# Low parts of the streamed weights: a VectorE subtraction replaced by a negated copy on ScalarE and an accumulating DMA

## The chip, the cores and the metric

One Trainium2 chip; the kernel uses one core. The metric is the device time of one execution in microseconds (us), taken as the median of several executions. Lower is better. Beside the times there is one profiled execution, and all durations below come from its trace. The compute engines are TensorE (PE in the profile, with its weight loads as a row of their own, PEld), VectorE (DVE), ScalarE (ACT) and GpSimd (POOL); SyncE (SP) issues most of the DMAs, and 16 DMA engines carry them out. Each engine has its own list of instructions, whose order is fixed when the program is built.

## The reference

Two layers of a diffusion trunk in float32, on 1024 latent tokens and 256 context tokens of width 1024. Layer 0 is multi-head latent attention with 8 heads, layer 1 a Hyena long convolution. Cut to what matters:

```python
for i in range(2):
    shift, scale, gate = split(silu(c) @ ada_w[i] + ada_b[i], 3)
    a = rmsnorm(x, norm_g[i]) * (1 + scale) + shift        # and the same for the context in layer 0
    if i == 0:   # latent attention
        cq, ckv, k_rope, g = split(a @ mla_w_in)
        q, kv = rmsnorm(cq) @ w_uq, rmsnorm(ckv) @ w_ukv
        y = (softmax(q k^T * s) v * silu(g)) @ mla_w_out
    else:        # Hyena
        u, g = split(a @ hy_w_in)
        v, g0, g1 = split(depthwise_conv3(u))
        z = g0 * longconv(v);  z = g1 * longconv(z)        # filters from a small MLP
        y = (z * silu(g)) @ hy_w_out
    x = x + gate * y
return rmsnorm(x, final_g)
```

The large products with weights are `a @ mla_w_in`, `@ mla_w_out`, `a @ hy_w_in` and `@ hy_w_out`. All weights arrive in float32.

## The kernel before

Everything is kept transposed: features on the 128 partitions, tokens along the row. A product that needs more precision than one pass of TensorE gives is made of three: every operand x is split into a high part hi (x rounded to the type fp32r) and a low part lo = x - hi (again fp32r), and the method `mm3` (lines 117 to 121) adds hi*hi, hi*lo and lo*hi in PSUM. So line 119 uses the weight's high part with the activation's high part, line 120 the weight's high part with the activation's low part, and line 121 the weight's low part. `split` (lines 95 to 97) makes the two parts of any operand: ScalarE copies (line 96), VectorE subtracts (line 97).

The weights of the four large products are not kept in SBUF; they are streamed in **pieces** of 128 x 512 float32, 256 KB (some 128 x 256). `feed` (lines 99 to 103) opens a pool and lists the pieces in the order in which they will be used; `weights` (lines 105 to 115) is called by whoever needs the next piece, and makes pieces ahead of it. For each piece it asks for three tiles: `raw`, called wr in the profile, and the two parts, called w. A tile name with n buffers takes them in turn; whoever writes a buffer waits until the last reader of its earlier content is done. Before the change wr has 2 buffers, and each of the parts has 3, or 2 in the pool that `out_first` opens. The load of `raw` goes on SyncE's queue (line 112). `weights` keeps at most two pieces listed as loaded, one of which it hands out.

The framework orders the instructions of each engine when the program is built, by priority (the order of the program text) and a model of when each is ready; an instruction whose buffer is not free yet can be placed behind later ones. So the place of a piece's instructions among others is not only that of the call.

There are three feeds:

- **Layer 0's input** (`layer0_in`, lines 440 to 623): 34 pieces of `mla_w_in` (wr<-in_w). Each tile of 128 output features takes two pieces; each piece of the latent tokens serves two halves of 512 tokens, 24 matmuls. `project` (lines 410 to 425) is a generator, and the work on it is interleaved with the making of the Hyena filters (`filters`, lines 284 to 358) and with the adaLN products (`ada`, whose loads of ada_w are called aw and pg). GpSimd loads the matrices of the filters' transforms here (line 295), and later ckv and krh for the attention (lines 641 to 647).
- **The output projection, first half of the tokens** (`out_first`, lines 886 to 905): 16 pieces of `mla_w_out` (wr<-in_wo). It begins inside the last unit of the attention, and each piece serves one half of the tokens, 12 matmuls. The pool has two buffers for each part. Its matmuls write tiles called po. The attention output is loaded and split by `out_heads` (lines 865 to 876, og<-ograw).
- **The rest** (`layer0_out` and `hyena`, lines 908 to 1272): the same 16 pieces of `mla_w_out` for the second half of the tokens (12 matmuls each), 64 pieces of `hy_w_in` (wr<-in_hw, 24 matmuls each, interleaved with the long convolutions of the chunk before), 16 pieces of the first six eighths of `hy_w_out` (wr<-in_hoa, 24 and 12 matmuls in turn) and 8 of the last two eighths (wr<-in_hob, 12 matmuls each, the first four for one half of the tokens, the last four for the other, with the final norm's first sums between). While the second half of the output projection runs, GpSimd loads the transform matrices dm in four steps (lines 966 to 970); each step first copies one element of x of the tile before last (line 969).

The attention between the first two feeds takes no streamed pieces; its weights (wa, wb, wc) go through `split`, which the change leaves as it is.

Of the kernel before, what the change touches and what calls it, by code (L numbers as in the profile page):

```python
# [11 lines left out]
F32 = mybir.dt.float32  # L12
F32R = mybir.dt.float32r
AF = mybir.ActivationFunctionType
ALU = mybir.AluOpType
# [4 lines left out]
P = 128  # L20
# [35 lines left out]
class Net:  # L56
# [47 lines left out]

    def weights(self):

        while self.coming and len(self.loaded) < 2:
            ap = self.coming.popleft()
            n = ap.shape[-1]
            raw = self.wp.tile([P, 512], F32, tag="wr", name="wr", bufs=2)[:, :n]  # L110
            hi, lo = [self.wp.tile([P, 512], F32R, tag=f"w{r}", name="w")[:, :n] for r in range(2)]
            self.nc.sync.dma_start(out=raw, in_=ap)
            self.split(raw, hi, lo)
            self.loaded.append((hi, lo))
        return self.loaded.popleft()

# [1299 lines left out]
```

## Time and profile before

| | |
|---|---|
| median of 3 executions | 1739.24 us (1736.87 to 1746.16) |
| the profiled execution | 1735.72 us |
| its span, first to last instruction | 1733.9 us |
| granted TensorE clock, mean | 0.976 of full speed |
| lines 96 and 97 on streamed pieces | 154 each, 93.7 and 102.4 us busy |

In the profile a group of instructions is given as line, engine, operation, output<-input by the program's names, the shapes and a count; then its busy time, the mean duration in ns, and how long its engine sat idle just before these instructions, with what ended most of that. A wait is given as "who, tile, line <- whom: us in total, times, longest". L96, L97 and L119 to L121 are helper lines that serve many tiles, so they are read together with the tile's name. The chain is the sequence of work that ended last, followed back from the last instruction. A line of the stage table gives start:end, length, busy us and count of PE, PEld, DVE, ACT and POOL, the granted clock, the busy share of the DMA engines and their GB/s.

The stages in the trace: layer 0's input from 0 to about 430 us, attention to about 931, the output projection to about 1037, the norm and the Hyena layer from there, of which the last output projection and the final norm take the part from about 1650.

### The profile page before, as it was taken

The page shows a single profiled execution, that of the slowest core. Times are in us where ns is not written, and L with a number is a line of the kernel's source. Part 1 is how long each engine was busy: PE and PEld are TensorE (multiplying, and loading weights), DVE is VectorE, ACT ScalarE, POOL GpSimd, SP SyncE. Part 2 cuts the span into 40 slices and gives each one's busy share as a digit, 9 for nine tenths or more (in the row PEclk, how much of TensorE's full clock was granted, in tenths as well). Part 3 has the DMA queues.
Part 4 walks back from the last instruction along what each step waited for, and adds up shares of the span by engine and source line. Part 5 has one row for each costly group of instructions (what it writes and reads, how often), then busy time and mean ns, then how long its engine had stood idle before and what let it go on. Part 6 is the DMA issues. An engine that isn't in the chain of part 4 may idle for free.

```text
span 1733.9 us, 22766 instructions
## 1 busy us (share of the span) xinstructions
PE 1635.3 (94%) x8096; PEld 1300.2 (75%) x8096; DVE 1442.4 (83%) x2539; ACT 766.1 (44%) x1331; POOL 15.4 (1%) x43
## 2 busy tenths in 40 slices
PE   6799897898999999999999999999999999999995
PEld 2467676686788788788787777888888888887873
DVE  4885978895598899899889466999999999999856
ACT  4533444435455555455556345433433433433313
POOL 1000000000000000000000010000000000000000
PEclk8899998999999999999999999999999999999998
DMA  9777563436101001010013781332332332334555
GB/s 341 255 231 222 182 191 118 147 95 196 37 22 42 25 26 37 25 33 25 19 56 121 233 268 64 101 97 84 100 117 83 104 111 85 102 113 138 175 158 204
DMA packets 139030, 207.19 MB, mean 119 GB/s; under 512 B 13386, under 2 KB 67361, under 8 KB 138788
## 3 DMA queue, kind: packets, MB, share of 16 engines
q1 hardware_dynamic: 135780, 195.05, 35.7%
q0 software_dynamic: 3136, 10.69, 1.9%
q8 instruction: 64, 1.05, 0.2%
q14 instruction: 50, 0.41, 0.1%
HBM read 149.97 MB, written 53.61 MB: 117 GB/s over the span
## 4 chain that ended last, share of the span: by engine, by line
PE 79%; DMA 8%; DVE 8%; ACT 3%; issue 1%; SPq 1%; DVEq 0%; ACTq 0%
PE pj L121 13%; PE pj L119 13%; PE pj L120 12%; PE O L120 2%; PE S L119 2%; PE O L119 2%; PE S L811 2%; DMA kd<-ko 2%; PE O L121 2%; PE apx L747 2%; PE S L810 2%; PE S L121 2%; PE S L120 2%; PE apx L748 2%; DMA aw<-in_adaw 2%; PE fu L119 2%
## 5 line engine op out<-in xcount | busy, mean ns | idle before, releaser
L96 ACT CAST w<-wr 128x512 fp32r<-128x512 f32 (+1 forms) x154 | 93.7, 609 | 259.2 <-PE pj L120 134.3
L119 PE MATMUL pj<-a,w 128*128 128x512 f32 x512 | 203.3, 398 | 1.7 <-ACT a L407 1.6
L121 PE MATMUL pj<-a,w 128*128 128x512 f32 x512 | 203.3, 398 | 0.0
L120 PE MATMUL pj<-a,w 128*128 128x512 f32 x512 | 203.2, 397 | 0.0
L813 ACT ACTIVATE p<-S 128x512 f32<-128x512 f32 x160 | 95.5, 597 | 148.2 <-DVE acc L820 69.5
L97 DVE TENSOR_TENSOR w<-wr,w 128x512 fp32r<-128x512 f32 (+1 forms) x154 | 102.4, 673 | 56.5 <-ACT w L96 56.3
L96 ACT CAST bh<-raw 128x512 fp32r<-128x512 f32 x128 | 77.0, 620 | 88.8 <-DVE raw L1056 71.1
L119 PEld LDWEIGHTS pj<-a,w 128*128 128x128 f32 x512 | 96.5, 189 | 22.0 <-ACT a L407 2.4
L120 PEld LDWEIGHTS pj<-a,w 128*128 128x128 f32 x512 | 96.6, 189 | 19.8 <-DVE a L408 0.2
L121 PEld LDWEIGHTS pj<-a,w 128*128 128x128 f32 x512 | 96.7, 189 | 19.4 <-issue 0.8
L97 DVE TENSOR_TENSOR p<-p 128x512 fp32r<-128x512 f32 x160 | 109.5, 685 | 1.5 <-ACT p L96 1.2
L749 DVE TENSOR_REDUCE cm<-apx 128x1 f32<-128x512 f32 (+1 forms) x192 | 107.3, 592 | 3.8 <-PE apx L748 3.0
L121 PE MATMUL pj<-pg,w 128*128 128x512 f32 (+1 forms) x248 | 98.0, 395 | 9.5 <-DVE w L97 9.5
L820 DVE TENSOR_TENSOR acc<-acc,p 128x512 f32<-128x512 f32 x144 | 98.9, 687 | 7.6 <-ACT p L813 6.7
L96 ACT CAST p<-p 128x512 fp32r<-128x512 f32 x160 | 99.4, 622 | 4.8
L119 PE MATMUL pj<-pg,w 128*128 128x512 f32 (+1 forms) x248 | 96.7, 393 | 2.4 <-ACT pg L407 2.4
L120 PE MATMUL pj<-pg,w 128*128 128x512 f32 (+1 forms) x248 | 98.1, 396 | 0.6 <-DVE pg L408 0.6
L97 DVE TENSOR_TENSOR bl<-raw,bh 128x512 fp32r<-128x512 f32 x128 | 84.9, 688 | 9.1 <-ACT bh L96 8.9
L119 PE MATMUL u<-bh,fm 128*128 128x256 f32 (+1 forms) x200 | 67.8, 340 | 11.6 <-ACT bh L96 9.0
L321 DVE TENSOR_TENSOR kk<-ph,dec 128x512 f32<-128x512 f32 x64 | 42.9, 685 | 35.4 <-DMA dec<-in_dec 28.2
L747 PE MATMUL apx<-kn,qn 128*128 128x512 f32 (+1 forms) x192 | 69.1, 364 | 2.3 <-DVE cm L749 1.9
L748 PE MATMUL apx<-krh,r 128*128 128x512 f32 (+1 forms) x192 | 67.2, 358 | 0.0
(304 smaller groups left out, 4392.4 us busy)
## 6 DMA issues: line engine op xcount, KB each, us to landing
aw<-in_adaw SPq DMA_DIRECT2D x32, 512.0 KB
kd<-ko SPq DMA_DIRECT2D x128, 128.0 KB
wr<-in_hw SPq DMA_DIRECT2D x64, 256.0 KB
kt<-kd SPq DMA_DIRECT2D x56, 256.0 KB
wr<-in_w SPq DMA_DIRECT2D x34, 256.0 KB
dec<-in_dec SPq DMA_DIRECT2D x64, 128.0 KB
pg<-in_adaw SPq DMA_DIRECT2D x32, 256.0 KB
wr<-in_wo SPq DMA_DIRECT2D x32, 256.0 KB
```

The source lines that it names most:

```text
L96: self.nc.scalar.copy(out=hi, in_=raw)
L97: self.nc.vector.tensor_tensor(out=lo, in0=raw, in1=hi, op=ALU.subtract)
L119: mm(out, lhsT=w[0], rhs=x[0], start=start, stop=False)
L120: mm(out, lhsT=w[0], rhs=x[1], start=False, stop=False)
L121: mm(out, lhsT=w[1], rhs=x[0], start=False, stop=stop)
L321: nc.vector.tensor_tensor(out=kk, in0=ps, in1=dec.broadcast_to([P, 2, 2, P]), op=ALU.mult)
L747: mm(b[:, :w], lhsT=qn[0][:, c], rhs=kn[0][:, o : o + w], start=True, stop=False)
L748: mm(b[:, :w], lhsT=r1[:, c], rhs=krh[:, o : o + w], start=False, stop=True)
L749: v.tensor_reduce(out=cm[:, t, i : i + 1], in_=b[:, :w], axis=AX.X, op=ALU.max)
L810: mm(S, lhsT=krh[:, c], rhs=r1, start=False, stop=False)
L813: act.activation(out=p, in_=S, func=AF.Exp, scale=ASCALE)
L820: v.tensor_tensor(out=acc, in0=acc, in1=p, op=ALU.add)
```

## The change

Only `weights` changes. It lists up to three pieces as loaded instead of two; `raw` has one buffer instead of two; and instead of calling `split`, ScalarE makes the high part as before and then a second rounded copy with the opposite sign, lo = -hi, from the same raw tile; a DMA on GpSimd's queue then adds the piece's float32 values from HBM onto lo, so that lo = x - hi. Each piece is thus read from HBM twice.

```diff
-        while self.coming and len(self.loaded) < 2:
+        while self.coming and len(self.loaded) < 3:
             ap = self.coming.popleft()
             n = ap.shape[-1]
-            raw = self.wp.tile([P, 512], F32, tag="wr", name="wr", bufs=2)[:, :n]
+            raw = self.wp.tile([P, 512], F32, tag="wr", name="wr", bufs=1)[:, :n]
             hi, lo = [self.wp.tile([P, 512], F32R, tag=f"w{r}", name="w")[:, :n] for r in range(2)]
             self.nc.sync.dma_start(out=raw, in_=ap)
-            self.split(raw, hi, lo)
+            self.nc.scalar.copy(out=hi, in_=raw)
+            self.nc.scalar.mul(out=lo, in_=raw, mul=-1.0)
+            self.nc.gpsimd.dma_start(out=lo, in_=ap, accum_op=ALU.add)
             self.loaded.append((hi, lo))
```

## Prediction

> **What bounds the kernel now.** I read the page first (engine totals, slices), then busy time by stage, then the waits of TensorE, then the weight pieces alone.
>
> ```profile
> span 1733.9 us, 22766 instructions
> PE 1635.3 (94%) x8096; PEld 1300.2 (75%) x8096; DVE 1442.4 (83%) x2539; ACT 766.1 (44%) x1331; POOL 15.4 (1%) x43
> q1 hardware_dynamic: 135780, 195.05, 35.7%
> q0 software_dynamic: 3136, 10.69, 1.9%
> ...
> 500.00:600.00 100.00, 100.00 (x484) 82.25 (x483) 88.49 (x144) 54.67 (x98) 0.00 (x0) 1.00 0.09 29
> 1130.00:1270.00 140.00, 139.14 (x723) 115.78 (x722) 133.29 (x228) 55.15 (x93) 0.00 (x0) 1.00 0.32 100
> 931.00:991.00 60.00, 55.45 (x229) 43.26 (x229) 39.00 (x58) 24.26 (x41) 0.00 (x0) 0.97 0.74 233
> 991.00:1037.00 46.00, 45.79 (x207) 34.92 (x206) 26.28 (x45) 22.60 (x38) 5.99 (x16) 1.00 0.78 256
> ```
>
> The stage rows give the length, then busy time of PE, weight loads, DVE, ACT and POOL, the granted clock, the DMA share and GB/s. VectorE is nearly full in the Hyena stage (133 of 140 us), but TensorE is fuller (139). The output projection of layer 0 (931 to 1037) is another kind of stage: VectorE has room there, and the DMA engines are 74 and 78% busy.
>
> Now who holds TensorE up (total us, times, longest): the two waits of the whole run that end with VectorE's low part, then all its waits between 1130 and 1555.
>
> ```profile
> PE pj L121 <- DVE w L97: 9.5, 4, 4.8
> PE po L121 <- DVE w L97: 1.4, 2, 1.1
> ...
> PE fu L119 <- ACT bh L96: 1.4, 3, 0.6
> PE fy L119 <- ACT bh L96: 0.8, 3, 0.3
> ```
>
> In 425 us of Hyena TensorE waits 2.2 us. The subtraction that goes is on TensorE's path for 10.9 us in all. That bounds the direct gain.
>
> **What is removed and added.** The pieces, and the loads by weight (count, KB each):
>
> ```profile
> L97 DVE TENSOR_TENSOR w<-wr,w 128x512 fp32r<-128x512 f32 x146 | 99.0, 686 | 51.7 <-ACT w L96 51.4
> L96 ACT CAST w<-wr 128x512 fp32r<-128x512 f32 x146 | 90.4, 620 | 238.7 <-PE pj L120 118.6 <-DMA wr<-in_hw 53.0 <-DMA wr<-in_w 21.8
> ...
> wr<-in_hw SPq DMA_DIRECT2D x64, 256.0 KB
> wr<-in_w SPq DMA_DIRECT2D x34, 256.0 KB
> wr<-in_wo SPq DMA_DIRECT2D x32, 256.0 KB
> ```
>
> VectorE loses the 146 subtractions of this row and 8 half-size ones. ScalarE gains as many negations; its copy of the same tile takes 0.62 us, so I take 0.62 for the negation and 154 x 0.62 = 95 us at most: 44% busy becomes 50%, no bound. The accumulating DMAs read all weights again, 146 x 0.262 + 8 x 0.131 = 39 MB. At the rate of the q0 row (10.69 MB in 1.9% of 1734 us, so 325 GB/s) that is 121 us of all 16 DMA engines, 7% of the span; twice that if reading the destination costs as much as reading the source.
>
> **The raw tile.** The diff also takes the raw tile from two buffers to one. Both ScalarE instructions read it, so the next load on SyncE's queue can be issued only after the negation, and nothing overlaps the load: a piece costs load + copy + negation in series. Loads seen (from the chain: start, us; the fourth row is TensorE's first low-part matmul of the output projection; then an issue and the cast that waited for it):
>
> ```profile
> 962.58 5.75 DMA wr<-in_wo
> 980.06 4.46 DMA wr<-in_wo
> 394.52 3.17 DMA wr<-in_w
> 938.13 0.50 PE po L121
> ...
> 1002.66 0.33 SPq L112 DMA_DIRECT2D wr<-in_wo  x1
> 1005.61 0.62 ACT L96 CAST w<-wr 128x512 fp32r<-128x512 f32 x1 [1.60 <-DMA wr<-in_wo]
> ```
>
> So 2.95 to 5.75 us. I take 3.8, the middle of the four, since slower consumption also thins the traffic. With 1.24 us on ScalarE the chain gives one piece every 5.0 us; ends 4.2 and 7.0. What TensorE needs:
>
> ```profile
> 959.82 0.39 PE L119 MATMUL po<-og,w 128*128 128x512 f32 x1
> 965.03 0.39 PE L121 MATMUL po<-og,w 128*128 128x512 f32 x1
> ...
> 1130.00:1270.00 140.00, 10.75 (x16) 9.95 (x16) 1.00 0.32 100
> ACT w L96 <- DMA wr<-in_wo: 20.5, 14, 4.0
> ```
>
> The first and last of 24 matmuls in a row give 5.21/23 = 0.227 us each. A piece of the output projection serves one half of the tokens: 12 matmuls, 2.7 us. The third row (VectorE's and ScalarE's instructions on raw tiles alone) shows 16 pieces in 140 us in Hyena, 8.75 us each. So Hyena covers 5.0 us, and the output projection does not: already with two raw tiles its casts waited 14 times for a load (last row, 931 to 1037).
>
> **The waits that are added.** SyncE waits for raw tiles already:
>
> ```profile
> SPq L112 <- DVE w L97: 237.3, 106, 17.3
> ```
>
> That wait moves to the negation. Behind it on SyncE stand the loads of attention output, residual x and kernel spectra; they were behind such a wait before, so I add nothing for them except at the far ends. ScalarE's copy waits for the raw load or the slot; behind it stand casts of attention output, the exponentials of the last attention unit and PSUM copies, and TensorE waits for those. GpSimd's DMA waits for the negation; behind it stand the loads of the DFT matrices. ScalarE's 0.62 us in front of a cast of bh can delay a Hyena transform, which the idle 85 of 140 us hide; uncovered it would be at most 64 x 0.62 = 40 us.
>
> **Output projection of layer 0, 32 pieces in 106 us.** About three pieces are made ahead (the third raw tile waits loaded; two slots are all that the first pool has). The first leaves TensorE at about 941 (its third matmul starts at 938.13), 10 us into the stage. Then 29 x 5.0 = 145 us, the last accumulating DMA and the last matmuls, 2.7 us. For the DMA the nearest rows are casting loads on the same queue (KB, us to landing):
>
> ```profile
> ckv<-ckv_d POOLq DMA_DIRECT2D x4, 640.0 KB, 7.5
> dm<-in_dm POOLq DMA_DIRECT2D x2, 320.0 KB, 3.4
> dm<-in_dm POOLq DMA_DIRECT2D x6, 512.0 KB, 5.2
> krh<-kr_d POOLq DMA_DIRECT2D x2, 320.0 KB, 13.0
> ```
>
> The 13.0 were queued behind the four loads of the first row, 2.6 MB, so I take 4 us; bounds 3 and 13. Sum 10 + 145 + 4 + 2.7 = 162 against 106: **+56 us**, ends +33 (4.2) and +114 (7.0). The new DMAs also queue on GpSimd behind the four pairs of DFT-matrix loads and the waits in front of them (x of the tile before last). Each is as long as about one piece, and lo is then late by that, which the third slot can absorb; I add nothing, 10 us at the far end.
>
> [...]
>
> **Hyena, 64 pieces.** Three slots, one in use, two ahead: lo must land within two pieces, 17.5 us, after copy, negation and landing of 1.24 + 4. Cover is ample: 0, between -2 (the 2.2 us of waits) and +10 if SyncE, whose raw loads queue among the kernel-spectrum loads, is late. The 11 us less of VectorE in each 140 us buy nothing, since TensorE stays at 139.
>
> **Layer 0's input, 34 pieces.**
>
> ```profile
> 60.00:180.00 120.00, 110.88 (x593) 80.03 (x594) 89.75 (x185) 51.44 (x95) 0.00 (x0) 0.96 0.67 207
> 168.52 0.62 ACT L96 CAST w<-wr 128x512 fp32r<-128x512 f32 x1 [0.19 <-PE pj L120]
> 173.96 0.62 ACT L96 CAST w<-wr 128x512 fp32r<-128x512 f32 x1 [4.33 <-PE pj L120]
> 179.40 0.62 ACT L96 CAST w<-wr 128x512 fp32r<-128x512 f32 x1 [1.24 <-PE pj L120]
> ```
>
> Bursts take a piece each 5.44 us, just above 5.0. The 8.9 MB more of traffic are 27 us of DMA time where the share is 0.67; I let a fifth of it show, since part of this stage waits for other loads, +6. Ends: -11 (the 9.5 us of waits gone, and some VectorE time) and +30 (all 27 us, and bursts at 6 us).
>
> **Last projection, 24 pieces.**
>
> ```profile
> 1650.00:1697.00 47.00, 46.06 (x207) 36.79 (x205) 26.44 (x42) 10.39 (x19) 0.00 (x0) 1.00 0.60 195
> 1697.12 10.37 SPq L112 DMA_DIRECT2D wr<-in_hob  x3
> ```
>
> The 16 of the first part alternate 24 and 12 matmuls, 5.4 and 2.7 us, close to the chain: +3. The last 8 are 2.7 us each; six of them come at 5.0 instead, +14, less some 6 us of norm between the two halves: +8. Together +11, ends 0 and +25.
>
> **Sum.** 56 + 0 + 6 + 11 = **+73 us**. On the profiled run, 1735.72 us (span 1733.9), that is 1809; this run lies 3.5 us below the median of 1739.24, so I forecast **1812 us**. Not all ends come together; low 33 - 2 - 11 + 0 = +20, so 1759; for the high end +114 and +30 of the rest, so 1883.
>
> **Rivals.**
> 1. *The accumulating DMA is late everywhere.* A slot turns once per three pieces, 26.2 us in Hyena, of which 8.75 are matmuls and 1.24 ScalarE: from a landing of 16 us on it sets the pace, and each us more costs 64/3 = 21 us. At 20 us: +85 in Hyena, and (1.24 + 20 + 2.7)/3 to /2 = 8 to 12 us a piece in the output projection, 32 x 10 = 320 for 106: about 2035. Against it: 3.4 and 5.2 us above. Chance 0.07.
> 2. *Faster: VectorE was the hidden bound.* Waits of 10.9 us go, and a few us at VectorE's chains in layer 0: 1739 - 14 = 1725. For it: 133 of 140. It decides only if the raw tile costs nothing, so if load and ScalarE fit into 2.7 us, a load of 1.5; the shortest row has 2.95. Chance 0.05.
> 3. *No change:* the added look-ahead hides the series, or the change does not do what it says where the pool has two slots and no third piece fits. 1739, within 8. Against it: look-ahead delays a chain slower than its user but does not speed it up, and 32 pieces outlast three. Chance 0.07.
>
> **How the numbers follow.** My case has 0.81, and its own range is 1759 to 1883. The range 1750 to 1885 holds it and leaves out the three rivals, 0.19. About 0.5% (8.7 us) is what a measurement of this kernel can tell from no change. Faster 0.05 is rival 2, same 0.07 is rival 3, slower is my case and rival 1, 0.88.
>
> **What would show it.** Right: between 931 and the end of the output projection some 160 us, with casts (L96's successor) spaced about 5 us and nearly all waiting for the load of wo; TensorE waiting there for ScalarE's high part or the DMA's low part, some 50 us; Hyena's period unchanged with VectorE about 122 of 140; q0 near 50 MB, landing in 3 to 5 us. Wrong: casts in the projection closer than 4 us, TensorE's waits at the new DMA in Hyena, or a shorter Hyena period.

## The result and the profile after

| | before | after |
|---|---|---|
| median, runs of the same chip | 1741.55 us (4) | 1860.84 us (4; 1852.85 to 1864.22) |
| ratio with its 95% interval | | 1.069 (1.066 to 1.072) |
| span of the profiled execution | 1733.9 us | 1857.6 us |
| granted TensorE clock, mean | 0.976 | 0.953 |

The change makes the kernel 6.9% slower, some 119 us. That lies inside the predicted range and 49 us above the predicted number. The page of after first: its span, TensorE's row, and the two kinds of DMA queue.

```profile
span 1857.6 us, 23064 instructions
PE 1679.1 (90%) x8096; PEld 1318.4 (71%) x8096; DVE 1358.5 (73%) x2385; ACT 846.2 (46%) x1487; POOL 150.8 (8%) x197
q1 hardware_dynamic: 135780, 195.05, 33.4%
q0 software_dynamic: 25312, 50.02, 15.1%
```

VectorE is busy for 84 us less and ScalarE for 80 more, the way that the diff says; overlapping instructions count once in these totals, so they are below the 102 us of the subtractions' own row. TensorE has the same 8096 matmuls, but is busy for 44 us longer. Where the time went is read from when the first and the last matmul of each stage's tiles start (us of each stage; the two halves of the output projection are the one with two slots and the one with three):

| stage | before | after | difference |
|---|---|---|---|
| layer 0's input | 446.5 | 461.2 | +14.7 |
| attention | 484.3 | 484.3 | 0 |
| output projection, first half | 60.3 | 95.7 | +35.4 |
| output projection, second half | 48.3 | 94.7 | +46.4 |
| norm and Hyena | 559.4 | 571.9 | +12.5 |
| last projection and final norm | 135.1 | 149.8 | +14.7 |

The stage rows of after: first half, second half, and one period of Hyena (length, busy us of PE, weight loads, DVE, ACT and POOL, clock, DMA share, GB/s).

```profile
945.00:1041.00 96.00, 67.25 (x232) 50.07 (x231) 28.76 (x40) 33.85 (x58) 14.86 (x17) 0.85 0.73 189
1041.00:1136.00 95.00, 63.00 (x225) 44.92 (x225) 17.93 (x31) 31.27 (x54) 18.90 (x30) 0.82 0.67 165
1244.00:1386.00 142.00, 141.59 (x737) 117.50 (x736) 127.42 (x215) 62.94 (x110) 14.01 (x16) 1.00 0.51 127
```

In the projection TensorE stands idle for 96 + 95 - 67.25 - 63.00 = 61 us, against 5 us before (106 - 55.45 - 45.79); and it is busy for 130 us instead of 101. So of the 85 us between these windows 56 are idle time and 29 are busy time. The windows do not hold quite the same work, 457 matmuls against 436: at 0.285 us of busy time each instead of 0.232, some 24 of the 29 us go with the lower granted clock (0.85 and 0.82), the other 5 are the 21 matmuls more. The waits of TensorE between 945 and 1136:

```profile
PE po L123 <- DMA w<-in_wo: 28.8, 11, 5.0
PE pj L123 <- DMA w<-in_wo: 27.7, 8, 6.8
PE pj L121 <- ACT w L113: 2.7, 2, 1.7
```

Nearly all end with the accumulating DMA, in both halves. The experiments show that this wait names the last link of a chain and not what sets its pace: a second raw tile takes most of it from the second half, the first half needs a third slot as well. The DMAs themselves (KB, median us from issue to landing):

```profile
wr<-in_wo SPq DMA_DIRECT2D x32, 256.0 KB, 3.2
w<-in_hw POOLq DMA_DIRECT2D x64, 256.0 KB, 4.8
w<-in_wo POOLq DMA_DIRECT2D x32, 256.0 KB, 5.4
```

How one turn runs in the second half, from the timeline of after (start, length, engine, line; in brackets how long the engine had been idle and what ended that; lines between are left out):

```profile
1075.52 6.45 SPq L112 DMA_DIRECT2D wr<-in_wo  x2
...
1080.46 0.62 ACT L113 CAST w<-wr 128x512 fp32r<-128x512 f32 x1 [4.46 <-DMA wr<-in_wo]
...
1086.43 0.63 ACT L114 ACTIVATE w<-wr 128x512 fp32r<-128x512 f32 x1
...
1087.86 0.33 SPq L885 DMA_DIRECT2D x_d<-x  x1
1087.90 1.30 POOL L971 CAST dm<-x 1x1 fp32r<-1x1 f32 x2 [5.12 <-DVE x L883]
...
1088.29 4.33 SPq L112 DMA_DIRECT2D wr<-in_wo  x2
...
1089.68 0.91 POOL L115 DMA_DIRECT2D w<-in_wo  x1
```

ScalarE sits 4.46 us with nothing to do until the raw load lands; the next two loads begin 12.77 us after these two (1075.52 and 1088.29), and only once SyncE has passed the store of the residual x. The negation that frees the raw tile had ended at 1087.06, so the store holds the load up for 1.2 us of the 12.77. GpSimd, too, issues an accumulating DMA behind a copy that had waited 5.12 us for x.

ScalarE's own order costs more. Later in this half its copy of a raw tile stands right behind a square of x for the norm (line 374), which waits until TensorE has finished the tile before:

```profile
1114.24 0.63 ACT L374 ACTIVATE sq<-x 128x512 f32<-128x512 f32 x1 [6.39 <-DVE x L883]
1114.78 0.60 ACT L113 CAST w<-wr 128x512 fp32r<-128x512 f32 x1
...
1125.45 0.63 ACT L374 ACTIVATE sq<-x 128x512 f32<-128x512 f32 x1 [5.63 <-DVE x L883]
1125.99 0.60 ACT L113 CAST w<-wr 128x512 fp32r<-128x512 f32 x1
```

The loads of these two pieces were issued at 1107.88 and 1119.85; at the 3.2 us that such a load takes, the copies could have begun 3.7 and 2.9 us earlier. So with one raw tile a late accumulating DMA can come back round: TensorE is late, so x is late, so the next copy is late, and with it the next load.

### The profile page after: what moved, and what is told of

Its sections match the earlier page's. It is cut to its first block, busy times and chain, and to the rows that moved or that the text cites. A ratio compares the mean times of both kernels' runs of the same rounds, so it can differ in the third digit from the quotient of the medians.

```text
span 1857.6 us, 23064 instructions
## 1 busy us (share of the span) xinstructions
PE 1679.1 (90%) x8096; PEld 1318.4 (71%) x8096; DVE 1358.5 (73%) x2385; ACT 846.2 (46%) x1487; POOL 150.8 (8%) x197
## 3 DMA queue, kind: packets, MB, share of 16 engines
q0 software_dynamic: 25312, 50.02, 15.1%
## 5 line engine op out<-in xcount | busy, mean ns | idle before, releaser
L815 ACT ACTIVATE p<-S 128x512 f32<-128x512 f32 x160 | 95.7, 598 | 148.7 <-DVE acc L822 68.4
L123 PEld LDWEIGHTS pj<-a,w 128*128 128x128 f32 x512 | 97.1, 190 | 24.6 <-DMA w<-in_hw 5.6
L115 POOL DMA_DIRECT2D w<-in_hw x64 | 56.0, 875 | 495.3 <-ACT w L114 452.5
L114 ACT ACTIVATE w<-wr 128x512 fp32r<-128x512 f32 (+1 forms) x154 | 95.0, 617 | 0.0
L115 POOL DMA_DIRECT2D w<-in_wo x32 | 28.0, 874 | 638.0 <-PE apx L750 480.0
```

The costliest lines, as they stand in the source:

```text
L114: self.nc.scalar.mul(out=lo, in_=raw, mul=-1.0)
L115: self.nc.gpsimd.dma_start(out=lo, in_=ap, accum_op=ALU.add)
L123: mm(out, lhsT=w[1], rhs=x[0], start=False, stop=stop)
L815: act.activation(out=p, in_=S, func=AF.Exp, scale=ASCALE)
```

## The experiments

The theory of the forecast (A) is the single raw tile: loads no longer overlap ScalarE's work. Against it stands the accumulating DMA (B): copy, negation, landing and use follow each other in every slot, and the number of slots divides the sum; where the two slots of the first half are meant, the expectations say S. A third question is whether a relieved VectorE gives anything back in Hyena. Ratios are against before, in runs on the same chip.

**Two raw tiles in after.**

```diff
-            raw = self.wp.tile([P, 512], F32, tag="wr", name="wr", bufs=1)[:, :n]
+            raw = self.wp.tile([P, 512], F32, tag="wr", name="wr", bufs=2)[:, :n]
```

> The changed kernel with two raw buffers again, all else as changed. Theory A (the single raw tile sets the pace where pieces are short): the second half of the output projection, which has three slots, falls from 94 us to 50-60, the first half, which has two slots, from 95 to 75-85 (two slots turn in 1.24 + 0.3 + 5.4 + 2.8 = 9.7 us, so 4.9 a piece); the last projection loses about 10 us; in all 55 to 75 us less than the changed kernel, so 1785 to 1805. Theory B (the landing of the accumulating DMA, 5 us in the middle, sets the pace, whatever the raw tile does): within 15 us of the changed kernel, 1845 to 1861, and TensorE still waits some 57 us for the low parts of wo.

Measured: 1816.77 us, 1.0442 (1.040 to 1.048). The stage rows of this kernel, first and second half, then its waits of TensorE in both:

```profile
947.00:1044.00 97.00, 70.11 (x231) 52.09 (x230) 28.85 (x40) 33.06 (x58) 14.92 (x17) 0.82 0.71 187
1045.00:1106.00 61.00, 52.96 (x216) 38.70 (x214) 17.73 (x31) 30.29 (x53) 18.96 (x31) 0.93 0.95 258
```

```profile
PE po L123 <- DMA w<-in_wo: 26.8, 9, 5.1
PE pj L123 <- DMA w<-in_wo: 7.8, 6, 2.8
```

The second raw tile takes the second half from 94.7 to 61.2 us and the wait there from 27.7 to 7.8, although that wait names the accumulating DMA. The first half stays where it was, 97.1 us after 95.7. So A holds with three slots and B with two; theory A's 50 to 60 us are just missed in the second half, its 75 to 85 clearly in the first. In the second half the DMA engines are now 95% busy (78% before); whether that is what keeps it 13 us over before was not tested. One turn of the first half in this kernel's timeline shows B's sum:

```profile
986.94 0.62 ACT L113 CAST w<-wr 128x512 fp32r<-128x512 f32 x1 [1.86 <-issue]
...
988.39 0.88 POOL L115 DMA_DIRECT2D w<-in_wo  x1 [2.13 <-ACT w L114]
...
998.09 0.62 ACT L113 CAST w<-wr 128x512 fp32r<-128x512 f32 x1 [0.57 <-PE po L122]
```

From one copy into a slot to the next copy into it pass 998.09 - 986.94 = 11.15 us: 1.45 until the DMA is issued, and 9.70 for its landing and the 12 matmuls that read the slot, after which the copy is released by TensorE. Here the median landing of the first half's DMAs is 7.0 us, as the view of this tile from 945 to 1041 us has it:

```profile
DMA to landing us min/median/max: 3.7/7.0/9.2
```

1.45 + 7.0 + 2.7 = 11.15; that the median gives this one turn to the hundredth is chance. Two slots give 5.6 us a piece, so 16 pieces take 89 of the 97 us.

**One raw tile in before.** The same line in before, `bufs=2` to `bufs=1`, and nothing else.

> The kernel before with one raw buffer instead of two; VectorE still subtracts, no added DMA. Theory A: load 3.2 + copy 0.62 + subtraction 0.69 + hand-overs 0.3 = 4.8 us a piece in series, 29 pieces at 4.8 instead of 3.3 in the output projection, so +40 to +50 there and up to +10 in the last projection: 1780 to 1800. Theory B: the raw tile does not matter, 1741 within 10.

Measured: 1821.65 us, 1.0473 (1.044 to 1.051): +84 us without any of the rest. Halves of the projection 78.5 and 70.8 us; the stage rows:

```profile
945.00:1022.00 77.00, 61.97 (x224) 41.78 (x223) 38.91 (x57) 24.51 (x42) 0.00 (x0) 0.96 0.56 182
1024.00:1095.00 71.00, 56.74 (x221) 38.48 (x219) 26.59 (x45) 24.11 (x40) 6.41 (x16) 0.93 0.52 165
```

The projection's +41 us is what theory A had, but the time is above its 1780 to 1800: Hyena became 20 us longer here (579.7), with a look-ahead of two (after, with three, lost 12.5), and layer 0's input 13 us. The DMA share fell to 0.56 and 0.52 from 0.74 and 0.78: the loads wait to be issued, not for bandwidth.

**The DMA without the addition.**

```diff
-            self.nc.gpsimd.dma_start(out=lo, in_=ap, accum_op=ALU.add)
+            self.nc.gpsimd.dma_start(out=lo, in_=ap)
```

> The changed kernel with the same DMA from the same queue, but without the addition: the low part is overwritten with the weights, so the product is another one; bytes, queue and waits are the same. If adding is what makes the landing long, it falls from 5.0 us in the middle to about 3.4 (the 320 KB casting load of before took 3.4) and the time by 20 to 50 us, to 1810-1840. If the bytes and the queue make it, landing and time stay: 5 us, 1850 to 1865.

Measured: 1812.77 us, 1.0422 (1.037 to 1.047). That is the first case: the landing falls to 3.4 us in Hyena, in the projection to 4.3. So the addition alone costs some 48 us of after: 15.4 and 11.9 in the two halves, 10.4 in layer 0's input, 7.8 in Hyena, 3.5 at the end. Queue, landings and the issuing instruction of this kernel, then that instruction in after:

```profile
q0 software_dynamic: 25312, 50.02, 9.5%
w<-in_hw POOLq DMA_DIRECT2D x64, 256.0 KB, 3.4
w<-in_wo POOLq DMA_DIRECT2D x32, 256.0 KB, 4.3
...
L115 POOL DMA_DIRECT2D w<-in_wo x32 | 16.9, 529 | 626.4 <-PE apx L750 480.4 <-ACT w L114 128.6 <-DMA w<-in_wo 9.2
```

```profile
L115 POOL DMA_DIRECT2D w<-in_wo x32 | 28.0, 874 | 638.0 <-PE apx L750 480.0 <-ACT w L114 142.3 <-DMA x_d<-x 7.7
```

The same bytes: less the 33 us of q0 before (1.9% of 1733.9), the 39.3 MB took 248 us of the 16 engines with the addition (15.1% of 1857.6 - 33) and 139 without (9.5% of 1808.7 - 33), 159 against 283 GB/s.

**Two raw tiles and the old look-ahead.** `bufs=2` as above, and `< 3` back to `< 2`: the negation and the DMA alone.

> The changed kernel with two raw buffers and a look-ahead of two pieces as before, so only ScalarE's negation and the accumulating DMA differ from the kernel before. With a landing of 5 us plus 1.5 for copy, negation and issue, a piece is begun one piece ahead instead of two, so TensorE would wait in the output projection about 6.5 - 2.8 = 3.7 us per piece if nothing else ran ahead: +100 us against before, 1840 or more. If the order that the framework makes runs ahead by itself as far as buffers are free, the look-ahead changes little: within 10 us of the run with two raw buffers and a look-ahead of three.

Measured: 1812.14 us, 1.0413 (1.038 to 1.045), the same as with the look-ahead of three within the intervals. One raw tile alone costs 84 us, the DMA path alone 74, both together 119 instead of 158: each hides part of the other.

**Three slots in the first half.**

```diff
-        self.feed([self.a["wo"][m] for m in range(KD)], 2, side)
+        self.feed([self.a["wo"][m] for m in range(KD)], 3, side)
```

> The changed kernel with three slots for each part in the first pool of the output projection instead of two; one raw buffer. Theory S (with two slots, a slot's turn of copy, negation, landing of the DMA and matmuls sets the first half's pace; the raw tile comes next): the first half falls from 95.7 us to about 78 to 84, where the kernel before with one raw buffer stood (78.5), the second half stays near 95, in all 1840 to 1850. Theory A (the raw tile alone): no part changes by more than 5 us, 1855 to 1866.

Measured: 1848.81 us, 1.0635 (1.061 to 1.067); first half 86.7 us, 9 less. That is the direction of theory S, but short of its 78 to 84; the second half came out at 89.8.

**Three slots and two raw tiles.** Both edits in after; to make room in SBUF the tile of the residual x in that pool (x1, line 906) has one buffer instead of two, which is an edit of its own.

> The changed kernel with two raw buffers and three slots in that pool; to make room the residual tile x1 there has one buffer instead of two. Theory S: both bounds of the first half are off, so it falls from 97 us (two raw buffers) to 65 to 75, the second half stays at 60 to 62; 1785 to 1797. If the first half is held by something else (the loads of the attention output, the DMA engines at 3/4 busy), it stays above 85 and the time above 1803.

Measured: 1804.90 us, 1.038 (1.035 to 1.041). First half 76.4 us, second 65.0: nearer to theory S than to the other, but above its halves and its time. The waits of TensorE in the projection, first and second half:

```profile
PE po L123 <- DMA w<-in_wo: 10.4, 5, 2.6
PE pj L123 <- DMA w<-in_wo: 9.0, 6, 5.9
PE po L121 <- DVE x L883: 4.4, 2, 2.3
```

For the first half a second raw tile alone gave nothing, a third slot alone 9 us, both 19. With both the wait for the DMA falls from 28.8 to 10.4 us there. The last row is new: matmuls wait until the residual is added, and VectorE waits for the load of x, so some of what is left is the price of the room.

**The same, without the addition** (the plain DMA of the third experiment).

> The run with two raw buffers and three slots in the first pool (1805 us), with the DMA made plain: without the addition the low part is overwritten with the weights, so the product is another one; bytes, queue and waits are the same. Theory (what is left of the loss there is the adding itself, its 5 to 6 us of landing and its time on the DMA engines): first half 76 to about 65, second half 65 to about 54, layer 0's input 459 to about 448, in all 30 to 45 us less, 1760 to 1775. If the bytes read twice make the rest, it stays within 15 us, 1790 to 1810.

Measured: 1778.03 us, 1.0208 (1.018 to 1.024); halves 73.0 and 60.0 us. The addition is worth 27 us here, a little less than expected; that ample slots and raw tiles cover part of its latency would fit, but was not shown. Still 24 us over the halves of before; TensorE waits here for x as well (6.5 us), and what makes the rest was not taken apart.

**The negation without the DMA.** Before with ScalarE's negation; VectorE then adds raw onto lo, so nothing is taken off VectorE.

```diff
-            self.split(raw, hi, lo)
+            self.nc.scalar.copy(out=hi, in_=raw)
+            self.nc.scalar.mul(out=lo, in_=raw, mul=-1.0)
+            self.nc.vector.tensor_tensor(out=lo, in0=raw, in1=lo, op=ALU.add)
```

> The kernel before, with two raw buffers and its look-ahead, where ScalarE makes the high part and the negated copy as in the change, and VectorE adds the raw tile onto the negated copy instead of subtracting; no added DMA. It prices ScalarE's 154 negations alone. Theory: ScalarE has room, 0 to +6 us, so within 0.5% of the kernel before. Rival: ScalarE's queue holds up casts for TensorE, +15 us or more.

Measured: 1756.04 us, 1.01 (1.008 to 1.012), so the rival's case. The projection is nearly as before (61.6 and 51.0 us); Hyena is 16 us longer. Its largest wait of TensorE there is for the cast of a transform's operand, not for a weight:

```profile
PE fy L121 <- ACT bh L96: 8.8, 3, 2.9
```

**The same, with a look-ahead of three** (`< 2` to `< 3`).

> The run with the negation and VectorE's addition, but no DMA (1756 us, Hyena 16 us longer), with a look-ahead of three pieces instead of two. Theory L (there the low part came too late, since copy, negation and addition follow one another one piece ahead): the third piece hides it and the time returns to within 0.5% of before, 1732 to 1748. Theory Q (the 0.62 us on ScalarE's queue stand in front of the casts that TensorE's transforms wait for, at a full VectorE): it stays at 1750 to 1760.

Measured: 1738.48 us, 0.9993 (0.998 to 1.001). The 16 us are gone, as theory L had it, with ScalarE as busy as in the last run (840.5 against 842.2 us). The same wait in Hyena:

```profile
PE fy L121 <- ACT bh L96: 0.9, 1, 0.9
```

So the negation costs nothing if it is done early enough. That with two pieces ahead it gets in front of the transform's casts on ScalarE fits both rows, but they make up half of the 16 us, and no run moved the casts alone.

**Before with a look-ahead of three**, nothing else.

> The kernel before with nothing but the look-ahead of three pieces. Pieces come in time before already (TensorE waits 10.9 us for low parts in the whole run), so within 0.5% of before, 1732 to 1748; if the 10.9 us of waits went, 1727 to 1731.

Measured: 1737.18 us, 0.9987 (0.997 to 1.001). The look-ahead by itself is worth nothing.

**The change in Hyena alone.** Before, with two raw tiles, and the negation, the DMA and the third piece ahead only for pieces 20 to 79 of the last feed, which are 60 of the 64 of Hyena.

```diff
+            if self.made in self.acc:      # acc=range(20, 80)
+                self.nc.scalar.copy(out=hi, in_=raw)
+                self.nc.scalar.mul(out=lo, in_=raw, mul=-1.0)
+                self.nc.gpsimd.dma_start(out=lo, in_=ap, accum_op=ALU.add)
+            else:
+                self.split(raw, hi, lo)
```

> The kernel before, with two raw buffers, and the negation, the accumulating DMA and the look-ahead of three only for 60 of the 64 pieces of the Hyena input weights; all other pieces are split as before. Theory: there the landing is hidden behind two pieces of matmuls and TensorE is the bound, so the 41 us (60 x 0.686) less of VectorE buy nothing: within 0.5% of before, 1730 to 1747. Rival (VectorE was the hidden bound there): its busy share falls by 11 us per 142 us, and the time by 10 to 25, to 1713-1728.

Measured: 1742.35 us, 1.0015 (1.000 to 1.003).

**The same pieces with neither negation nor addition**: after the copy comes only a plain DMA into lo.

> As the run with the change for 60 Hyena pieces alone, but there neither ScalarE's negation nor the addition: the low part of those pieces is overwritten with the weights by a plain DMA, so the product is another one. It frees VectorE of 60 subtractions and adds nothing to ScalarE. Theory (TensorE is the bound in Hyena): period 141 to 142 us as before, in all within 0.5%, 1732 to 1748. Rival (VectorE's relief is worth something that ScalarE's negation eats up again): period under 139, 10 us or more off the time, 1715 to 1730.

Measured: 1744.10 us, 1.002 (1.000 to 1.004). One period of Hyena in this kernel and, below, in the one before it:

```profile
1147.00:1289.00 142.00, 140.79 (x733) 116.48 (x732) 125.93 (x214) 53.75 (x92) 8.44 (x16) 1.00 0.43 128
```

```profile
1145.00:1286.00 141.00, 140.81 (x733) 117.00 (x732) 126.34 (x214) 62.35 (x109) 13.97 (x16) 1.00 0.51 129
```

VectorE is 9 us less busy in each period than before (135.28 of 142 there), ScalarE is as before in the first and 8 us busier in the second, and the period stays at 141 to 142 us: TensorE fills it. In Hyena the relief of VectorE buys nothing, and the new path costs at most 0.3%.

## Why the prediction was right, and where its sizes were off

**Right: direction, place and mechanism.** VectorE was not the bound: Hyena's period did not shorten with VectorE at 127 of 142 us (forecast 122 of 140). From the fourth store of g_d (line 1052, in after 1054) in one period to that in the next it is 142.2 and 141.4 us before, 141.8 and 145.1 in after. The output projection lost most, 82 of the 119 us, and there the single raw tile takes part, as the second half of the run with two raw tiles shows. q0 moved 50.02 MB as worked out; the last projection gave +14.7 for a forecast of +11.

**Mis-sized: the output projection, +82 for +56.** The first term that came out wrong is "the last accumulating DMA": its landing was put at 4 us and counted once, at the end. It measured 5.4 us in after and 7.0 in the first half with two raw tiles, and it stands in every turn of a slot. With the plain DMA, which lands in 4.3 us, the projection is 163.1 us long, +54.5, close to the forecast; the 27 us on top go with the addition. The forecast's own formula, written down only for the first rival, would have shown the risk: (1.24 + landing + 2.7)/2 is 4.0 us a piece at 4 us, hidden under the 5.0 of the raw chain, 4.7 at 5.4, and 5.5 at 7. So the forecast's 5.0 us a piece was the pace of one of two chains, and the two interleave: in the first half of after ScalarE's copies waited 11 times for a raw load (23.8 us) and 6 times for the slot (17.1). Together 190 us for 32 pieces, 5.9 each.

**The raw chain itself** was taken as load + copy + negation, 5.0 us. In the second half of after the 14 copies from 1044.44 to 1129.80 come 6.6 us apart, and with the plain DMA 5.9. Two terms are missing, both of them places in a queue. On ScalarE three copies stand behind squares of x, which the engine reaches after idle times of 6.39 and 5.63 us, as shown above, and of 9.02 us at 1067.87, whose cause the profile does not show. On SyncE three loads are issued about 1 us late behind stores and loads of x, 3 us in all. Besides, two loads took 6.5 and 7.2 us until their copy began, instead of 3.8. "I add nothing for them" was wrong in direction: not only is what stands behind the raw tile's work late, but the raw tile's work behind the rest. No run moved either place alone.

**The addition's traffic.** Of the two guesses the doubled one, 242 us, had the right size: 248 us of the 16 engines, against 139 without the addition. That reading the destination makes the difference was not shown. No stage was priced with it; the plain DMA shows 48 us, more than half of them in the projection.

**TensorE's clock was not in the sum.** The forecast counted idle time, and its 56 us happen to equal the idle time that came. The 24 us of slower matmuls came on top. The two don't simply add up as causes: where the raw chain sets the pace, faster matmuls would only wait longer; where the slot turn does, they are part of it.

**Layer 0's input, +14.7 for +6**, inside its bounds. Three comparisons put the addition there at 7 to 11 us (461.2 - 450.8 with one raw tile; 463.1 and 459.3, less 452.0, with two), one raw tile alone at 13. These too overlap, and single executions of unchanged code there differ by up to 3.7 us (445.7 to 449.4).

**Hyena, +12.5 for 0 (bound +10).** By the same stores of g_d, 5.5 us of it lie before the first of them, 4.9 in the periods and 2.1 behind the last. At the start TensorE waits twice for the accumulating DMA of hw, at 1143.81 for 1.5 us and at 1161.38 for 3.2; the forecast had named such a wait as a sign of being wrong, and these two are all that came. The Hyena-only run shows +0.6, so it is not the steady state; the run with two raw tiles keeps 9.2 of it and the plain DMA 4.7. What makes the rest is left open.

**The rivals.** The late DMA (16 us in Hyena, 20 in that rival's sum) didn't come: no run shows such a landing as the median of a stage. The largest is the 7.0 us above, and in after all these DMAs have a median of 5.0 us and a longest of 13.8. Nor is it much longer where VectorE is fuller: its median is 4.8 us over all of Hyena and 5.5 in the period from 1244 to 1386 us, where VectorE is busy 127 of 142 us, and 5.4 in the projection, where it is busy 47 of 191. The faster rival needed a VectorE bound, which the two Hyena runs exclude: their intervals begin at 1.000. The rival of no change said that look-ahead hides the series: in the projection it doesn't.

## What to carry to other kernels

Moving work off an engine is worth what that engine holds up and no more: read it from the waits of the engine that is full, here 10.9 us, before paying for it with a buffer or a DMA. For a streamed operand write down each chain that must turn once per piece: raw tile (issue, load, readers) over its buffers, and slot (make, landing, use) over its slots; the largest sets the pace at best, a latency inside a slot counts every turn, and work that stands in front of a link in its engine's queue belongs to the chain. A wait names the link that came last: whether a buffer or a latency is behind it is told by adding a buffer, and where two causes hide each other, only by adding both.

## What the runs showed of the hardware

- The DMA that adds into SBUF is a dearer thing here than the same DMA without the addition: 159 against 283 GB/s of the 16 engines, 4.8 against 3.4 us to landing in Hyena and 5.4 against 4.3 in the projection, and 874 against 529 ns of GpSimd for the issue. The two runs with two raw tiles and three slots agree, with q0 shares of 15.3% with the addition and 9.6% without.
- In the projection of after longer stalls cost twice. After such a wait for the DMA matmuls run at nearly half speed for a while. From the timeline of after, the first three and the last two of ten in a row:

```profile
1062.66 0.80 PE L123 MATMUL pj<-og,w 128*128 128x512 f32 x1 [6.82 <-DMA w<-in_wo]
1063.26 0.63 PE L121 MATMUL pj<-og,w 128*128 128x512 f32 x1
1063.68 0.63 PE L122 MATMUL pj<-og,w 128*128 128x512 f32 x1
...
1066.19 0.39 PE L122 MATMUL pj<-og,w 128*128 128x512 f32 x1
1066.42 0.39 PE L123 MATMUL pj<-og,w 128*128 128x512 f32 x1
```

They start 0.43 us apart for some 3 us, then 0.23: after a wait of 6.82 us the eight steps from 1062.66 to 1066.19 took 3.53 us instead of 1.8. Of the 19 waits for this DMA in the projection of after, all 11 of 2.5 us and more are followed by such a stretch, at once or after a few matmuls; of the 8 of 2.1 us and less, 7 are not. One of these:

```profile
1075.94 0.50 PE L123 MATMUL pj<-og,w 128*128 128x512 f32 x1 [1.34 <-DMA w<-in_wo]
1076.27 0.39 PE L121 MATMUL pj<-og,w 128*128 128x512 f32 x1
1076.49 0.40 PE L122 MATMUL pj<-og,w 128*128 128x512 f32 x1
```

The stretches last 3.1 to 5.2 us where no new wait cuts them short, and the stage rows of the two halves have a clock of 0.85 and 0.82, that of Hyena's period 1.00. What starts and ends such a stretch was not taken apart.
- Extra work for ScalarE of 76 us (842.2 against 766.1) costs 16 us with two pieces ahead (1756.04 us, ratio 1.01) and nothing with three (1738.48 us, 0.9993), although the look-ahead alone is worth nothing (1737.18 us, 0.9987).
